# Two-layer hybrid decoder on one core: order of work at the borders of its stages, rewritten

## The chip, the cores and the metric

The kernel runs on one core of a Trainium2 chip. The metric is the device time of one execution in microseconds (us). The engines are TensorE (PE; its weight loads are PEld), VectorE (DVE), ScalarE (ACT), GpSimd (POOL) and SyncE (SP), which issues most of the transfers.

## The reference

Two layers act on 512 tokens of width 1024; inputs and output are float32.

```
for l in range(2):
    x = x + 0.5 * swiglu(rmsnorm(x, ffn1_norm[l]), ffn1_w13[l], ffn1_w2[l])
    z = rmsnorm(x, mix_norm[l]) @ w_in[l]     # pool input | mLSTM q,k,v,o,i,f | attention q,k,v | 3 gates
    y_a = pooling(z); y_b = mLSTM(z); y_c = differential attention(z), with rope tables from positions
    x = x + (sum_b sigmoid(gate_b) * (y_b @ P_b)) @ w_out[l]
    x = x + 0.5 * swiglu(rmsnorm(x, ffn2_norm[l]), ffn2_w13[l], ffn2_w2[l])
return rmsnorm(x, final_norm)
swiglu(h, w13, w2) = (silu(g) * u) @ w2, with g, u = split(h @ w13); the hidden width is 2816 = 22 tiles of 128
```

## The kernel before

x lies in eight tiles of 128 channels by 512 tokens. Every large product is made of three matmuls in a float32 form of reduced precision (`k3`, L341 to L343: hi by hi, hi by lo, lo by hi). So each tile of weights that a transfer brings is split in two: the high part is a cast on ACT (L264), the low part a subtraction on DVE (L265). `weight` hands out the next weight in TensorE's order, splits those that are due within 7 us of TensorE's time, and starts the loads of those due within 16 us (L252 and L257 issue them on SP's queue). Split weights lie in the tiles w (plain), V (forms, below) and dh, dl (down projection, loaded to dr).

There are four FFNs. TensorE's order in one is written out by `ffn_plan`. Of the 22 hidden tiles the first five are plain pairs ("u": a product with g's weights, one with u's). From the sixth on, a pair is computed on halves of the token range and of the weights with seven products instead of eight ("a" to "d", `pair_a` to `pair_d`). Their weights are sums and differences of g's and u's weights (`f1` to `f4`, made by the additions L287 on DVE and then split). Between the pairs lie the products with w2 of the part of hidden tiles before ("D", which update x at L741). The last FFN ends with "E", `finish`: two halves of the tokens, each normed and sent out while the other is computed.

An RMSNorm goes like this. Each updated tile of x is split (L439 on ACT, L440 on DVE) and squared (L452 on ACT), and the squares are added up on POOL (L453, seven additions per norm). TensorE sums over channels (L469), POOL takes the power -1/2 (L461), TensorE spreads the result over the partitions (L516), and ACT copies it to R (L502). The products are started with the unnormed x, and R is multiplied in afterwards: `plain_pair` does so for g (L661), applies silu (L662), does so for u (L665), multiplies u by g on POOL (L666), and splits the result (L651 on ACT, L652 on DVE). R also makes the operands of the forms (`operands`, L479 to L483).

`pair_a` copies its products out of PSUM on ACT (L677, L680). The third block of a pair reuses the PSUM tile that L677 empties.

`tables` makes the rope tables, a mask and the attention's lambdas once, at the end of the first FFN: some 30 operations, most of them on DVE (L573 to L639), issued in one go. The mixer weaves its own small steps between products with w_in; `merge_stream` takes the sigmoids of the gates (L1212) and splits y (L1218 on ACT, L1219 on DVE) before the products with P_b.

TensorE's order is as written. The order on the other engines is chosen when the program is built, from priorities (splits of weights have a high one) and estimated times. At the start, `WARM` matmuls on constants (L544) run ahead of the first weight.

Of the kernel before, what the change touches and what calls it, by code (L numbers as in the profile page):

```python
# [41 lines left out]
WARM = 12  # L42
# [5 lines left out]
PARTS = ((0, 5), (5, 10), (10, 14), (14, 18), (18, 22))  # L48
# [4 lines left out]
def ffn_plan(end):  # L53
# [17 lines left out]
    plan.append(("x", 0, 0))  # L71
# [43 lines left out]
class Trunk:  # L115
# [3 lines left out]
    def __init__(self, ctx, tc, a, out):  # L119
# [7 lines left out]
        self.plan = None  # L127
# [115 lines left out]
    def load_weight(self, i):  # L243
# [4 lines left out]
        if kind in ("p", "d"):  # L248
            _, nk, n = src.shape
            raw = self.wtile() if kind == "p" else self.t([P, 640], "dr", 3)  # L250
            raw = raw[:, : nk * n].rearrange("p (k n) -> p k n", k=nk)
            self.nc.sync.dma_start(raw, src)  # L252
            self.wraw[i] = raw
        elif kind == "f1":
            for c in ("u", "g"):
                raw = self.wtile()
                self.nc.sync.dma_start(raw.rearrange("p (k n) -> p k n", k=KD), src[c])  # L257
                src[c] = raw

# [55 lines left out]
    def weight(self):  # L315
# [10 lines left out]
        for k, at in ahead:  # L326
            if at < 7.0:
                self.split_weight(k)
        for k, at in ahead:
            self.load_weight(k)  # L330
# [53 lines left out]

    def behind(self, ins):
# [46 lines left out]
    def split_x(self, m, gcol, dve=False):  # L432
        nc = self.nc
        g = self.vec[:, gcol + m : gcol + m + 1]
        xh, xl = self.act(dt=F32R), self.act(dt=F32R)
        if dve:
            nc.vector.tensor_scalar(out=xh, in0=self.x[m], scalar1=g, scalar2=None, op0=ALU.mult)
        else:
            nc.scalar.activation(xh, self.x[m], AF.Copy, scale=g)  # L439
        nc.vector.scalar_tensor_tensor(  # L440
            out=xl, in0=self.x[m], scalar=g, in1=xh.bitcast(F32), op0=ALU.mult, op1=ALU.subtract
        )
        self.xs[m] = (xh, xl)

    def square(self, m):
# [7 lines left out]
        nc.gpsimd.tensor_tensor(out=self.ssq, in0=self.ssq, in1=sq, op=ALU.add)  # L453
# [68 lines left out]
    def setup(self):  # L522
# [25 lines left out]
        for m in range(KD):  # L548
            self.split_x(m, V_FFN1, m % 2 == 0)
            if m == 0:  # L550
# [3 lines left out]
        self.split_weight(1)  # L554

    def tables(self):

        nc, a, c = self.nc, self.a, self.const

# [3 lines left out]
        def load(out, in_):  # L563
            self.order(nc.gpsimd.dma_start(out, in_), self.last_pool)
# [16 lines left out]
        self.mqb = self.t([P, P], "mqb", dt=BF16)  # L581
        self.behind(nc.vector.tensor_copy(self.mqb, mq[:, :P]))
# [4 lines left out]
        lv = lam.rearrange("p (l i d) -> p l i d", l=L * 2, i=2)  # L587
        self.behind(nc.vector.tensor_tensor(out=pr, in0=lv[:, :, 0, :], in1=lv[:, :, 1, :], op=ALU.mult))
        sm = self.t([P, L * 2], "lsum")
# [13 lines left out]
        ang = y()  # L603
        self.behind(nc.vector.tensor_copy(ang, pos))
        nc.vector.tensor_scalar(out=ang, in0=ang, scalar1=c[:, C_INV : C_INV + 1], scalar2=None, op0=ALU.mult)
# [8 lines left out]
        n1, n2, s1, kk = y(), y(), y(), y()  # L614
        nearest(n1, ang, 2.0**-20)
        axpy(ang, n1, -(2.0**20), ang)
        nearest(n2, ang, 2.0**-9)
        axpy(ang, n2, -(2.0**9), ang)
        nc.vector.tensor_scalar(out=s1, in0=n1, scalar1=BIG_1, scalar2=None, op0=ALU.mult)
        axpy(s1, n2, MID_1, s1)  # L620
        nc.vector.tensor_tensor(out=kk, in0=s1, in1=ang, op=ALU.add)
        nearest(kk, kk, 1.0 / TWO_PI)
        axpy(s1, kk, -PI_1, s1)
        nc.vector.tensor_tensor(out=ang, in0=ang, in1=s1, op=ALU.add)
        axpy(ang, kk, -PI_2, ang)
        axpy(ang, n2, MID_2, ang)
        axpy(ang, n1, BIG_2, ang)
        nc.vector.tensor_scalar(out=s1, in0=n1, scalar1=BIG_3, scalar2=None, op0=ALU.mult)
        axpy(s1, n2, MID_3, s1)
        axpy(s1, kk, -PI_3, s1)  # L630
        nc.vector.tensor_tensor(out=ang, in0=ang, in1=s1, op=ALU.add)
        nc.vector.tensor_scalar(out=ang, in0=ang, scalar1=PI_F, scalar2=-PI_F, op0=ALU.min, op1=ALU.max)
        self.cos = self.t([P, T], "cos")
        self.sin = self.t([P, T], "sin")
        nc.scalar.activation(s1, ang, AF.Sin)
        nc.vector.tensor_scalar(out=self.sin, in0=s1, scalar1=c[:, C_SGN : C_SGN + 1], scalar2=None, op0=ALU.mult)
        nc.scalar.activation(kk, ang, AF.Sin, scale=0.5)
        nc.scalar.activation(kk, kk, AF.Square)
        nc.vector.tensor_scalar(out=self.cos, in0=kk, scalar1=-2.0, scalar2=1.0, op0=ALU.mult, op1=ALU.add)  # L639
# [15 lines left out]
    def plain_pair(self, xs, act):  # L655
# [59 lines left out]
    def ffn(self, gnext, extra=None):  # L715
# [6 lines left out]
        for kind, p, j in ffn_plan(gnext == V_FIN):  # L722
            if kind == "u":
                yield from self.plain_pair(xs, acts[0])
            elif kind == "a":
                pairs[j] = yield from self.pair_a()
# [6 lines left out]
            elif kind == "x":  # L733
                if extra is not None:
                    extra()
# [390 lines left out]
    def pool_mix(self, l, c):  # L1126
        nc = self.nc
        pw = self.t([P, P], "pw", 2)
        nc.sync.dma_start(pw, self.a["pool_w"][l, c])
# [77 lines left out]
    def merge_stream(self, l):  # L1207
        nc = self.nc
        for m in range(KD):
# [5 lines left out]
        ys = []  # L1215
        for c in range(KD):
            yh, yl = self.act(dt=F32R), self.act(dt=F32R)
            nc.scalar.copy(yh, self.y[c])  # L1218
# [176 lines left out]
```

## Time and profile before

| | us |
|---|---|
| median of 3 runs | 2291.49 |
| lowest, highest | 2288.96, 2293.58 |
| the profiled execution | 2286.44 |
| its span, first to last instruction | 2284.6 |
| TensorE busy | 2218.4 (97%) |
| VectorE busy | 1581.7 (69%) |
| ScalarE busy | 1020.4 (45%) |
| GpSimd busy | 234.0 (10%) |
| mean granted clock of TensorE | 0.988 |

The table is of one profiled execution but for its first two lines; that execution lies 0.2% below the median. TensorE's granted clock is 1 at 2.4 GHz and 0.5 at 1.2 GHz.

### The profile page before, as it was taken

The page shows a single profiled execution, that of the slowest core. Times are in us where ns is not written, and L with a number is a line of the kernel's source. Part 1 is how long each engine was busy: PE and PEld are TensorE (multiplying, and loading weights), DVE is VectorE, ACT ScalarE, POOL GpSimd, SP SyncE. Part 2 cuts the span into 40 slices and gives each one's busy share as a digit, 9 for nine tenths or more (in the row PEclk, how much of TensorE's full clock was granted, in tenths as well). Part 3 has the DMA queues.
Part 4 walks back from the last instruction along what each step waited for, and adds up shares of the span by engine and source line. Part 5 has one row for each costly group of instructions (what it writes and reads, how often), then busy time and mean ns, then how long its engine had stood idle before and what let it go on. Part 6 is the DMA issues. An engine that isn't in the chain of part 4 may idle for free. (4 is left out here: it accounts for less than half of the span.)

```text
span 2284.6 us, 33195 instructions
## 1 busy us (share of the span) xinstructions
PE 2218.4 (97%) x13116; PEld 1944.4 (85%) x13116; DVE 1581.7 (69%) x2426; ACT 1020.4 (45%) x1717; POOL 234.0 (10%) x183
## 2 busy tenths in 40 slices
PE   8999998999999999999999999999999999999997
PEld 6899997887787888999988999988887778899997
DVE  6876777757845577777677777665686465877775
ACT  4444453534453344444443444454344534444444
POOL 3100002001201320000020000010120032100002
PEclk8999999999999999999999999999999999999999
DMA  4333331313222333333224333222222223333323
GB/s 154 122 100 100 98 102 35 97 60 106 83 81 79 122 105 117 109 95 100 83 85 131 99 103 97 84 62 84 84 92 83 83 96 108 126 105 97 101 70 102
DMA packets 76524, 219.43 MB, mean 96 GB/s; under 512 B 9256, under 2 KB 11832, under 8 KB 76368
## 3 DMA queue, kind: packets, MB, share of 16 engines
q1 hardware_dynamic: 73648, 214.29, 30.0%
q10 hardware_dynamic: 2496, 2.43, 0.3%
q8 instruction: 102, 1.67, 0.3%
q0 software_dynamic: 224, 0.60, 0.1%
q14 instruction: 54, 0.44, 0.1%
HBM read 210.97 MB, written 2.11 MB: 93 GB/s over the span
## 5 line engine op out<-in xcount | busy, mean ns | idle before, releaser
L341 PE MATMUL mx<-A,V 128*128 128x256 f32 x1632 | 457.0, 280 | 11.7 <-ACT A L677 11.7
L343 PE MATMUL mx<-A,V 128*128 128x256 f32 x1632 | 457.8, 280 | 1.4 <-DVE V L265 1.3
L341 PE MATMUL mm<-A,w 128*128 128x512 f32 x1120 | 450.9, 403 | 7.2 <-DVE x L741 3.7
L342 PE MATMUL mx<-A,V 128*128 128x256 f32 x1632 | 456.2, 280 | 0.0
L342 PE MATMUL mm<-A,w 128*128 128x512 f32 x1120 | 440.5, 393 | 4.1 <-DVE A L1219 1.9
L343 PE MATMUL mm<-A,w 128*128 128x512 f32 x1120 | 441.0, 394 | 2.0 <-DVE w L265 2.0
L265 DVE TENSOR_TENSOR V<-w,V 128x1024 fp32r<-128x1024 f32 (+1 forms) x272 | 295.5, 1105 | 159.1 <-PE mx L342 96.8
L264 ACT CAST V<-w 128x1024 fp32r<-128x1024 f32 (+1 forms) x272 | 256.5, 943 | 272.3 <-issue 98.0
L341 PEld LDWEIGHTS mx<-A,V 128*128 128x128 f32 x1632 | 306.3, 188 | 17.6 <-ACT A L677 12.5
L342 PEld LDWEIGHTS mx<-A,V 128*128 128x128 f32 x1632 | 307.9, 189 | 4.4
L343 PEld LDWEIGHTS mx<-A,V 128*128 128x128 f32 x1632 | 307.5, 188 | 2.0 <-DVE V L265 2.0
L264 ACT CAST w<-w 128x1024 fp32r<-128x1024 f32 (+2 forms) x166 | 172.4, 1039 | 295.5 <-PE mm L342 94.2
L265 DVE TENSOR_TENSOR w<-w,w 128x1024 fp32r<-128x1024 f32 (+2 forms) x166 | 209.8, 1264 | 107.4 <-ACT w L264 107.0
L342 PE MATMUL mm<-A,dh 128*128 128x512 f32 (+1 forms) x736 | 281.0, 382 | 2.5 <-DVE A L652 2.5
L343 PE MATMUL mm<-A,dl 128*128 128x512 f32 (+1 forms) x736 | 279.9, 380 | 0.9 <-DVE dl L265 0.8
L341 PE MATMUL mm<-A,dh 128*128 128x512 f32 (+1 forms) x736 | 280.6, 381 | 0.0
L341 PEld LDWEIGHTS mm<-A,w 128*128 128x128 f32 x1120 | 213.1, 190 | 52.3 <-ACT w L264 4.2
L342 PEld LDWEIGHTS mm<-A,w 128*128 128x128 f32 x1120 | 213.1, 190 | 49.7 <-DVE A L1219 3.6
L343 PEld LDWEIGHTS mm<-A,w 128*128 128x128 f32 x1120 | 212.2, 189 | 48.1 <-DVE w L265 2.5
L264 ACT CAST dh<-dr 128x512 fp32r<-128x512 f32 (+1 forms) x168 | 111.0, 661 | 244.4 <-PE mm L342 117.9
L741 DVE SCALAR_TENSOR_TENSOR x<-mm,x 128x512 f32<-128x512 f32 x152 | 104.5, 688 | 121.3 <-PE mm L343 121.3
L343 PEld LDWEIGHTS mm<-A,dl 128*128 128x128 f32 x736 | 138.4, 188 | 28.3 <-DVE dl L265 1.7
(236 smaller groups left out, 3272.8 us busy)
## 6 DMA issues: line engine op xcount, KB each, us to landing
w<-in_w13a SPq DMA_DIRECT2D x88, 512.0 KB, 3.5
w<-in_w13b SPq DMA_DIRECT2D x88, 512.0 KB, 3.4
w<-in_w_fm SPq DMA_DIRECT2D x76, 512.0 KB, 3.4
dr<-in_w2b SPq DMA_DIRECT2D x56, 256.0 KB, 2.6
dr<-in_w2a SPq DMA_DIRECT2D x48, 256.0 KB, 2.6
dr<-in_w2a SPq DMA_DIRECT2D x32, 320.0 KB, 2.9
dr<-in_w2b SPq DMA_DIRECT2D x32, 320.0 KB, 2.9
w<-in_w_p SPq DMA_DIRECT2D x16, 512.0 KB, 3.4
```

The lines of the kernel that those rows point to most:

```text
L264: self.last_hi = nc.scalar.copy(hi, raw)
L265: self.last_lo = nc.vector.tensor_tensor(out=lo, in0=raw, in1=hi.bitcast(F32), op=ALU.subtract)
L341: nc.tensor.matmul(ps, wh, xh, start=start, stop=False, skip_group_check=more)
L342: nc.tensor.matmul(ps, wh, xl, start=False, stop=False, skip_group_check=more)
L343: nc.tensor.matmul(ps, wl, xh, start=False, stop=stop, skip_group_check=more)
L741: nc.vector.scalar_tensor_tensor(out=self.x[m], in0=ps, scalar=0.5, in1=self.x[m], op0=ALU.mult, op1=ALU.add)
```

## The change

It has these parts, and leaves the arithmetic as it was but for where it is done.

1. `WARM` goes from 12 to 20.
2. `PARTS` goes from parts of 5, 5, 4, 4, 4 hidden tiles to 5, 4, 4, 4, 5.
3. `weight` looks up to 23 us ahead: while a plain weight is used, forms due within 13 us are split and those due within 23 us loaded. Of plain and down weights no more than two at a time, the one in use among them, are split, and no more than three loaded.
4. All loads of weights are tied to one order, that of use (`fetch`); the pooling weights' load comes behind the last of them.
5. The sums of squares (`square`) and the product u by g of a plain pair (`take_u`) move from POOL to DVE.
6. At the start, the first weight's low part comes behind three tiles of x instead of five, and the last ones behind it (`order`).
7. `tables` becomes a generator whose steps are issued at least 1.6 us of TensorE's planned time apart, from the first pair of the last part on, instead of at once behind the last pair.
8. `merge_stream` splits y before it takes the sigmoids.

```diff
-WARM = 12
+WARM = 20
-PARTS = ((0, 5), (5, 10), (10, 14), (14, 18), (18, 22))
+PARTS = ((0, 5), (5, 9), (9, 13), (13, 17), (17, 22))
-    plan.append(("x", 0, 0))
+    def fetch(self, out, in_):
+
+        d = self.nc.sync.dma_start(out, in_)
+        if self.last_load is not None:
+            self.order(d, self.last_load)
+        self.last_load = d
...
-        ahead, at = [], self.pe_time(i)
+        kind = self.wsrc[i][0]
+        plain = kind == "p"
+        split, load, at = [], [], self.pe_time(i)
+        seen = {"p": 0, "d": 0}
+        seen[kind] = 1
         for k in range(i + 1, len(self.wsrc)):
-            if at > 16.0:
+            if at > 23.0:
                 break
-            ahead.append((k, at))
+            nxt = self.wsrc[k][0]
+            if nxt in ("p", "d"):
+                seen[nxt] += 1
+                if at < 7.0 and seen[nxt] <= 2:
+                    split.append(k)
+                if at < 16.0 and seen[nxt] <= 3:
+                    load.append(k)
+            else:
+                if at < (13.0 if plain else 7.0):
+                    split.append(k)
+                if at < (23.0 if plain else 16.0):
+                    load.append(k)
             at += self.pe_time(k)
...
+    def steps(self, gen, us=1.6):
+
+        if next(gen, self) is not self:
+            self.defer(us, lambda: self.steps(gen, us))
...
-        nc.gpsimd.tensor_tensor(out=self.ssq, in0=self.ssq, in1=sq, op=ALU.add)
+        nc.vector.tensor_tensor(out=self.ssq, in0=self.ssq, in1=sq, op=ALU.add)
...
-            self.split_x(m, V_FFN1, m % 2 == 0)
-            if m == 0:
+            self.split_x(m, V_FFN1, m % 2 == 0, self.last_lo if m > 2 else None)
+            if m == 2:
                 self.split_weight(0)
...
+        yield
         nearest(n1, ang, 2.0**-20)
+        yield
         axpy(ang, n1, -(2.0**20), ang)
+        yield
...
             nc.vector.tensor_tensor(out=u, in0=ps, in1=self.R, op=ALU.mult)
-            self.last_pool = nc.gpsimd.tensor_tensor(out=u, in0=u, in1=g, op=ALU.mult)
+            nc.vector.tensor_tensor(out=u, in0=u, in1=g, op=ALU.mult)
             self.gated(u, g, act)
...
             elif kind == "a":
+                if extra is not None and j == PARTS[-1][0]:
+                    self.steps(extra())
...
     def merge_stream(self, l):
         nc = self.nc
+        ys = []
+        for c in range(KD):
+            yh, yl = self.act(dt=F32R), self.act(dt=F32R)
+            nc.scalar.copy(yh, self.y[c])
+            nc.vector.tensor_tensor(out=yl, in0=self.y[c], in1=yh.bitcast(F32), op=ALU.subtract)
+            ys.append((yh, yl))
         for m in range(KD):
             for br in range(3):
                 g = self.gates[m, br]
```

The lines behind the changed ones move down: L265 becomes L271, L287 becomes L293, L661, L665 and L666 become L722, L726 and L727, L652 becomes L713, L741 becomes L801, and L608, L609 and L612 become L651, L652 and L655. Three places show what the change moves on DVE.

In the first FFN, where the plain pairs end, DVE's rows before are these: the last pair's R multiplied in (L661, L665), with the forms' sums (L287) and low parts (L265, tiles V) around them, up to the split of the last pair (L652).

```order
L661 TENSOR_TENSOR V_569<-mm_578,R_272 128x512
L287 TENSOR_TENSOR w_608<-w_608,w_574 128x512
L265 TENSOR_TENSOR V_605<-w_574,V_605 128x512
L287 TENSOR_TENSOR w_574<-w_574,w_576 128x512
L265 TENSOR_TENSOR V_612<-w_608,V_611 128x1024
L287 TENSOR_TENSOR w_576<-w_574,w_608 128x512
L265 TENSOR_TENSOR V_654<-w_574,V_653 128x1024
L287 TENSOR_TENSOR w_759<-w_663 128x512
L665 TENSOR_TENSOR V_569<-mm_617,R_272 128x512
L287 TENSOR_TENSOR w_759<-w_759,w_661 128x512
L265 TENSOR_TENSOR V_708<-w_576,V_707 128x1024
L652 TENSOR_TENSOR A_645<-V_569,A_644 128x512
```

At the same place after the change, from the last pair's g on:

```order
L722 TENSOR_TENSOR V_581<-mm_596,R_280 128x512
L726 TENSOR_TENSOR V_581<-mm_636,R_280 128x512
L271 TENSOR_TENSOR V_625<-w_490,V_624 128x1024
L713 TENSOR_TENSOR A_578<-V_483,A_577 128x512
L293 TENSOR_TENSOR w_962<-w_840 128x512
L271 TENSOR_TENSOR V_734<-w_492,V_733 128x1024
L293 TENSOR_TENSOR w_962<-w_962,w_838 128x512
L727 TENSOR_TENSOR V_581<-V_581 128x512
L713 TENSOR_TENSOR A_664<-V_581,A_663 128x512
```

The sums and low parts of the first forms now stand ahead of the last pair's g; between u (L726) and the product u by g (L727), which POOL did before, stand five other rows.

In the second FFN the same place was before as in the first, but for one addition (L287) that stood ahead of L661. After the change DVE's rows there, again from the last pair's g on, are these:

```order
L722 TENSOR_TENSOR V_7710<-mm_7725,R_7377 128x512
L271 TENSOR_TENSOR V_7754<-w_7642,V_7753 128x1024
L293 TENSOR_TENSOR w_7919<-w_7763 128x512
L726 TENSOR_TENSOR V_7710<-mm_7765,R_7377 128x512
L293 TENSOR_TENSOR w_7919<-w_7919,w_7761 128x512
L727 TENSOR_TENSOR V_7710<-V_7710 128x512
L271 TENSOR_TENSOR V_7863<-w_7644,V_7862 128x1024
L713 TENSOR_TENSOR A_7793<-V_7710,A_7792 128x512
```

Here only one row (L293) stands between L726 and L727.

In the last part of the first FFN, DVE's rows after the change have the tables' steps (L651, L652, L655; tiles cos and sin serve as scratch) among the pairs' work; before, all of them stood behind the last pair, among the last updates of x and their splits.

```order
L713 TENSOR_TENSOR A_2897<-A_2677,A_2896 128x512
L651 TENSOR_SCALAR A_2839<-cos_2775 128x512
L271 TENSOR_TENSOR V_2942<-w_2938,V_2941 128x1024
L652 TENSOR_SCALAR A_2839<-A_2839 128x512
L801 SCALAR_TENSOR_TENSOR x_8_78<-mm_2905,x_8_78 128x512
L655 SCALAR_TENSOR_TENSOR cos_2775<-A_2839,cos_2775 128x512
L271 TENSOR_TENSOR V_3001<-w_2821,V_3000 128x1024
L667 TENSOR_SCALAR sin_2776<-A_2838 128x512
L762 TENSOR_TENSOR A_2844<-A_2844,mm_2947 128x256
L293 TENSOR_TENSOR w_3269<-w_3157 128x512
```

One or two steps of the tables now stand between every two pieces of the pairs' work.

## Rows read from the trace of the kernel before

**Rows 1.** The page's first part: busy time, share of the span and instructions of each engine.
```profile
PE 2218.4 (97%) x13116; PEld 1944.4 (85%) x13116; DVE 1581.7 (69%) x2426; ACT 1020.4 (45%) x1717; POOL 234.0 (10%) x183
```

**Rows 2.** The waits of PE: line, for what; us in total, times, longest.
```profile
PE mx L341 <- ACT A L677: 11.7, 4, 4.1
PE mm L341 <- ACT A L821: 5.8, 2, 2.9
PE mm L341 <- DVE x L741: 3.7, 1, 3.7
...
PE mx L341 <- ACT A L1218: 3.0, 2, 1.6
PE mm L341 <- DVE mif L801: 3.0, 4, 1.3
...
PE mx L469 <- POOL A L1263: 2.9, 1, 2.9
```

**Rows 3.** Windows of half clock: us; PE, PEld, DVE, ACT, POOL busy; PEclk, DMA, GB/s.
```profile
10.50:17.30 6.80, 4.77 (x12) 3.65 (x12) 6.73 (x9) 5.07 (x9) 1.55 (x1) 0.50 0.76 293
27.60:34.40 6.80, 6.08 (x18) 5.17 (x19) 1.33 (x2) 1.04 (x1) 2.64 (x2) 0.50 0.33 109
85.60:89.00 3.40, 3.40 (x16) 3.40 (x17) 2.72 (x6) 1.51 (x3) 0.00 (x0) 0.50 0.65 155
...
389.40:396.20 6.80, 6.80 (x21) 5.54 (x21) 1.31 (x2) 0.08 (x1) 1.96 (x1) 0.50 0.21 62
...
sum 44.20, PE 41.45 PEld 35.89 DVE 25.54 ACT 22.57 POOL 7.42; mean PE 4.15 PEld 3.59 DVE 2.55 ACT 2.26 POOL 0.74
```

**Rows 4.** Timeline of the start: start, us, instruction [idle before <- releaser].
```profile
9.92 0.50 PE L341 MATMUL mm<-A,w 128*128 128x512 f32 x1 [3.30 <-ACT w L264]
...
12.70 0.80 PE L343 MATMUL mm<-A,w 128*128 128x512 f32 x1 [2.03 <-DVE w L265]
...
15.75 12.51 POOL L453 TENSOR_TENSOR ssq<-ssq,A 128x512 f32<-128x512 f32 x7 [14.49 <-ACT A L452]
...
19.89 2.31 DVE L265 TENSOR_TENSOR w<-w,w 128x1024 fp32r<-128x1024 f32 x1
...
36.67 0.59 ACT L502 COPY R<-mx 128x512 f32<-128x512 f32 x1 [6.62 <-PE mx L516]
```

**Rows 5.** Timeline of the first FFN's border from plain pairs to forms.
```profile
77.36 0.68 DVE L265 TENSOR_TENSOR V<-w,V 128x512 fp32r<-128x512 f32 x1
78.08 0.69 DVE L287 TENSOR_TENSOR w<-w,w 128x512 f32<-128x512 f32 x1
78.69 1.22 DVE L265 TENSOR_TENSOR V<-w,V 128x1024 fp32r<-128x1024 f32 x1
79.82 0.68 DVE L287 TENSOR_TENSOR w<-w,w 128x512 f32<-128x512 f32 x1
...
82.99 1.58 POOL L666 TENSOR_TENSOR V<-V 128x512 f32<-128x512 f32 x1 [8.72 <-DVE V L665]
...
84.60 0.62 ACT L651 CAST A<-V 128x512 fp32r<-128x512 f32 x1 [2.96 <-POOL V L666]
...
85.54 0.56 PE L341 MATMUL mx<-A,V 128*128 128x256 f32 x1 [4.14 <-ACT A L677]
```

**Rows 6.** Timeline of the same border in the third FFN.
```profile
1205.15 0.69 DVE L287 TENSOR_TENSOR w<-w 128x512 f32<-128x512 f32 x1 [1.62 <-DMA w<-in_w13a]
...
1215.26 0.48 PE L341 MATMUL mx<-A,V 128*128 128x256 f32 x1 [4.13 <-ACT A L677]
```

**Rows 7.** Windows from R to the border and around the tables, columns as in rows 3.
```profile
37.30:76.60 39.30, 39.30 (x175) 32.53 (x174) 35.49 (x59) 20.04 (x31) 8.33 (x4) 1.00 0.31 108
297.00:356.00 59.00, 58.69 (x397) 54.04 (x396) 41.06 (x66) 26.42 (x44) 1.61 (x3) 1.00 0.30 92
356.00:390.00 34.00, 27.55 (x110) 20.86 (x109) 31.25 (x50) 17.32 (x28) 11.85 (x12) 0.94 0.08 23
```

**Rows 8.** Timeline of ACT in the first mixer, where TensorE waits for L821.
```profile
450.63 1.04 ACT L264 CAST w<-w 128x1024 fp32r<-128x1024 f32 x1 [6.02 <-PE mm L342]
451.69 1.28 ACT L1047 ACT_TABLE_LOAD   x1
```

**Rows 9.** Timeline of the end: ACT's queue issues stores.
```profile
2267.54 2.80 ACTq L1293 DMA_DIRECT2D out<-A  x4
```

More of the change, by code (lines that the diff above doesn't have):

```diff
@@ L319, in weight @@
         self.split_weight(i)
-        ahead, at = [], self.pe_time(i)
+        kind = self.wsrc[i][0]
[3 more added lines that the diff above has]
+        seen[kind] = 1
         for k in range(i + 1, len(self.wsrc)):
-            if at > 16.0:
+            if at > 23.0:
                 break
-            ahead.append((k, at))
+            nxt = self.wsrc[k][0]
[10 more added lines that the diff above has]
+                    load.append(k)
             at += self.pe_time(k)
[L326 to L329, printed above, removed]
+        for k in split:
+            self.split_weight(k)
+        for k in load:
             self.load_weight(k)
@@ L430, in prep, with split_x @@
         self.square(m)
-    def split_x(self, m, gcol, dve=False):
+    def split_x(self, m, gcol, dve=False, after=None):
         nc = self.nc
@@ L435, in split_x @@
         xh, xl = self.act(dt=F32R), self.act(dt=F32R)
+        vec = []
         if dve:
-            nc.vector.tensor_scalar(out=xh, in0=self.x[m], scalar1=g, scalar2=None, op0=ALU.mult)
+            vec.append(nc.vector.tensor_scalar(out=xh, in0=self.x[m], scalar1=g, scalar2=None, op0=ALU.mult))
         else:
-            nc.scalar.activation(xh, self.x[m], AF.Copy, scale=g)
-        nc.vector.scalar_tensor_tensor(
+            self.last_xh = nc.scalar.activation(xh, self.x[m], AF.Copy, scale=g)
+        vec.append(nc.vector.scalar_tensor_tensor(
             out=xl, in0=self.x[m], scalar=g, in1=xh.bitcast(F32), op0=ALU.mult, op1=ALU.subtract
-        )
+        ))
+        if after is not None:
+            for v in vec:
+                self.order(v, after)
+        self.last_xl = vec[-1]
         self.xs[m] = (xh, xl)
@@ L554, in setup @@
         self.split_weight(1)
+        self.order(self.last_hi, self.last_xh)
+        self.order(self.last_lo, self.last_xl)
     def tables(self):
         nc, a, c = self.nc, self.a, self.const
+        tick = self.t([P, 16], "rsv", 2)[:, 0:1]
+        done = nc.gpsimd.tensor_tensor(out=tick, in0=self.x[0][:, 0:1], in1=self.x[0][:, 0:1], op=ALU.add)
         def y(shape=(P, T), dt=F32):
@@ L563, in load @@
         def load(out, in_):
-            self.order(nc.gpsimd.dma_start(out, in_), self.last_pool)
+            self.order(nc.gpsimd.dma_start(out, in_), done)
         gb = self.t([P, L * 8], "gb")
@@ L602, in tables @@
         load(pos, a["positions"].partition_broadcast(P))
-        ang = y()
+        self.cos = self.t([P, T], "cos")
+        self.sin = self.t([P, T], "sin")
+        ang, s1 = self.cos, self.sin
+        yield
+        yield
         self.behind(nc.vector.tensor_copy(ang, pos))
+        yield
         nc.vector.tensor_scalar(out=ang, in0=ang, scalar1=c[:, C_INV : C_INV + 1], scalar2=None, op0=ALU.mult)
@@ L1128, in pool_mix @@
         pw = self.t([P, P], "pw", 2)
-        nc.sync.dma_start(pw, self.a["pool_w"][l, c])
+        self.order(nc.sync.dma_start(pw, self.a["pool_w"][l, c]), self.last_load)
         pm = self.ps("mx")
@@ L1214, in merge_stream @@
                     self.order(si, e)
[L1215 to L1218, printed above, removed]
-            nc.vector.tensor_tensor(out=yl, in0=self.y[c], in1=yh.bitcast(F32), op=ALU.subtract)
-            ys.append((yh, yl))
         mg = []
```

34 lines of the change are left out of this document (25 added, 9 removed).

## The prediction

> **What bounds the kernel now.** The page's first part comes first: TensorE is busy for 2218.4 us of the span of 2284.6, VectorE for 1581.7, and the others for less than half [rows 1]. So TensorE sets the time, and at most two things can be had without fewer columns: its 66.2 us of idle time (2284.6 less 2218.4), and what the half clock costs it. For the first I read the waits of PE. They are not many small ones: five lines carry the larger part, each with a few long waits [rows 2]. For the second I read windows of the stretches at a granted clock of 0.50, the 1.2 GHz level. Ahead of the tail there are ten, 44.2 us in all [rows 3]; half of that, 22.1 us, is what they cost. Each begins during or behind a wait, or several close together. Then I looked at the places one by one, in the timeline. All lie at borders: the start, the step from plain pairs to forms, the end of the first FFN, the mixer's gates, the merge, and the tail.
>
> **The start and the first border.** Here the chain runs through DVE, so I add up the chain and not the gaps. TensorE waits 3.30 us for the first weight's cast and 2.03 us for its low part [rows 4]; both stretches at half clock, from 10.5 and 27.6, belong here [rows 3]. POOL adds the squares in 12.51 us, 1.79 each, and a DVE operation beside it took 2.31 us where its like takes 1.22 [rows 4, 5]. R is ready at 37.26. What an addition takes on DVE itself the rows of the forms' sums and low parts show, which also read two tiles in SBUF: 0.61 from start to start for 512 columns, 1.13 for 1024 [rows 5]; so an estimate for 256 wide is 0.35 and for 640 wide 0.74. In the change POOL's 12.51 us become seven times 0.61, or 4.3 us, R no longer waits for POOL's sums, and the low part comes two positions earlier. I take R at 28, since the third weight's loads and TensorE's sums still stand ahead of it (27 to 31). The eight further warm matmuls fill the 3.30 us and start nothing earlier; they cost up to 0.2 us.
>
> From R to the last pair's g, the order of the changed kernel has on DVE 43 operations of 512, 7 of 1024, 20 of 256 and 2 of 640: 26.2 + 7.9 + 7.0 + 1.5 = 42.6 us. Before, DVE was busy for 35.49 of 39.30 us there, from 37.3 to 76.6, and POOL for 8.33 [rows 7]; TensorE needs no more than those 39.3, so the stretch is now DVE's. It ends at 70.6. From there to the end of L727 there are five of 512 and two of 1024, 5.3 us, then the cast of the result, 0.5, and the copy L738, 0.3 (starts 84.60, and TensorE going on at 85.54, bound the two at 0.94 [rows 5]). The third block of the first pair would start at 76.8 where it started at 85.54 [rows 5]. That is 8.7; for the bounds, R at 27 and no slip give 10, R at 31 gives 5.7, and a slip on top 5. I take **8**.
>
> **The other borders.** L677 is waited for four times, 11.7 us in all, 4.14 and 4.13 of it in the first and third FFN [rows 2, 5, 6], which leaves 3.4 for the second and fourth. POOL's product there starts 8.72 us after its last (so it is not POOL that is full): it comes late since u's turn on DVE lies behind sums and low parts, and the cast L651 and the copy L677 stand behind it on ACT [rows 5]. In the change, from u on DVE does u, one sum and the product, 3 x 0.61, and ACT's cast and copy 0.9: 2.7 us, against two blocks of twelve matmuls that TensorE has left; sixteen such took 3.40 us at half clock [rows 3], so 24 at full clock take 2.6. The wait goes nearly to nothing: **2.5** of 3.4 (bounds -2 and 3.4; below nothing if the longer look-ahead makes DVE late). In the third FFN the sums began late, as DVE waited 1.62 us for a transfer of g or u [rows 6]; loads up to 23 us ahead take that away. The wait of 4.13 and half of the stretch of 3.4 at half clock behind it are 5.8; I take **5** (2 to 5.8).
>
> **The tables.** From 356 to 390 TensorE is busy for 27.55 of 34 us, so 6.45 are idle, 3.7 of them for x at L741, which stands behind the tables on DVE [rows 2, 7]; two stretches of half clock, 3.4 and 6.8 us [rows 3], cost 5.1. In the last part, 297 to 356, DVE is busy for 41.06 of 59 us [rows 7]. The tables' 27 steps at about 0.61 are 16.5 us: 57.6 of 59. They fit there, barely, among splits that `weight` asks for up to 7 us ahead. What stays is the last x's way through split and square, 1.5 us. I take **10** of 11.5 (6 to 11.5).
>
> **Mixer, merge, tail.** L821 is waited for 2.9 us in each layer [rows 2]: ACT does a cast of 1.04 us and then loads a table, 1.28 us, ahead of it, having been idle for 6.02 us [rows 8]. In the changed order the table's load comes ahead of the cast, in that idle time: 1.3 per layer. The gates' wait for mif, 3.0 in all [rows 2], shrinks by about a microsecond per layer, as DVE takes mif ahead of a low part. Against that, the output of v on DVE (mv) now stands behind two or three reciprocals; I price that at 0.6 per layer. Together **3.5** (-2, if mv is waited for longer, to 8, if all waits and the half clock behind them go). Splitting y first changes less than it says: the cast of y needs free tiles and comes behind the same transfer, and only one moves ahead of one sigmoid; of 3.0 us [rows 2] I take **1** (0 to 2). At the end, four stores hold ACT for 2.80 us [rows 9] and PE waits 2.9 for what is behind them [rows 2]; with five hidden tiles in the last part instead of four a tile of output takes 15 matmuls instead of 12, at 0.11 us each 1.6 instead of 1.3 us, the stores spread out, and **1.8** is won (0 to 2.9). For waits that a new order of loads and splits makes elsewhere I take off **2** (0 to 8).
>
> **The sum.** 8 + 2.5 + 5 + 10 + 3.5 + 1 + 1.8 - 2 = 29.8. Against the profiled execution, 2286.4, that is 2256.6; it stood 5.1 below the median of the runs, so 2261.7, or 2262.
>
> **Rivals.** First, DVE becomes the bound at more than the first border. For it speak 57.6 of 59 us in the last part and 42.6 us behind R; against it, that 42 sums and 20 products on POOL no longer slow DVE beside them, which cost about 1.1 each [rows 4, 5]. If R comes at 31 and DVE is 5 us behind, the first border gives nothing; if the tables exceed 17.9 us (59 less 41.06), low parts of forms come late and 6 of 10 go; with 2 at the other borders 16 are lost: 2278.
>
> Second, the clock falls again behind the waits that are left. In the trace it fell behind 3.30 us of idle time [rows 3, 4] and behind 4.14 [rows 3, 5]; how short a wait leaves it alone no row shown tells, and some of one to two microseconds stay. If the stretches of the first FFN's end and the third border stay, 5.1 and 1.7 are not won: 2269. The Trainium skill, "TensorE: Matmul & The Clock Gate", section "What's actually happening", says that how many matmuls run at the half clock differs from run to run of one kernel, since the monitor's window runs freely; no run here shows it yet, and by it eight further warm matmuls are no promise of a full clock.
>
> Third, it ends slower: all loads of weights now stand in one order on SP's queue, and a load of w2 that waits for a free dr tile, which DVE's low part frees, holds the loads of w13 behind it. With 17 form pairs in each of four FFNs, 68, slower by over 0.2% needs 34.4 us more than my forecast, or 0.51 us for each pair. Against it: in the steady part DMA is at 0.30 and TensorE idle for 0.3 of 59 us [rows 7], so there is slack. I put it at 2300.
>
> Fourth, the change does not do what it says: waits at one border move to the next, since TensorE's order stays; the time stays near 2290.
>
> **How the numbers follow.** Within 0.2%, 4.6 us, counts as the same. The forecast, 2250 to 2268, gets 0.58; the first rival 0.16, the second 0.12, the third 0.07, the fourth 0.07. Faster: 0.58 + 0.16 + 0.12 = 0.86; same 0.07; slower 0.07. The range goes from 2246, where all upper bounds hold (43.6 us), to 2281, which takes in the first two rivals.
>
> **What would show it.** Right: no wait for L453's successor at the first sums of squares; a third block that starts near 77; no x waited for near 375; waits for L738 under a microsecond in the last three FFNs; fewer than six stretches at half clock; the table load of L1107 ahead of a cast. Wrong: waits for low parts of V (L271) in the last part of the first FFN or within the pairs, DVE busy without a pause ahead of them; SP's queue holding w13's loads; waits for mv; half clock behind waits of one or two microseconds.

## The result, and the profile after

The changed kernel takes 2258.92 us in the median of 4 runs (2256.43 to 2260.04), against 2291.92 of before beside it: a ratio of 0.9856, with a 95% interval of 0.9839 to 0.9873. The profiled execution takes 2259.48 us, with a span of 2257.7 us, 26.9 less than before; the medians differ by 33.0, as the profiled execution of the kernel before lay 5.5 us below its median. The forecast was 2262, with 2246 to 2281 as its range.

The page's first part, for [rows 1]: POOL has lost 98 us, DVE gained only 12.4 though it took over 62 operations, and TensorE's busy time fell by 12.8. Most of it is that TensorE runs less at half clock: half of the difference between its busy time in those stretches, 41.45 us before [rows 3] and 18.34 after (below), is 11.6, an estimate.

```profile
PE 2205.6 (98%) x13148; PEld 1937.6 (86%) x13148; DVE 1594.1 (71%) x2488; ACT 1018.0 (45%) x1716; POOL 136.0 (6%) x122
```

The waits of PE in the changed kernel, for [rows 2]; L738 is what was L677, L881 was L821, L1272 was L1218, L483 was L453, L1323 was L1263:

```profile
PE mx L361 <- ACT A L738: 10.5, 4, 7.0
PE mm L361 <- ACT A L881: 7.0, 2, 3.5
...
PE mx L361 <- ACT A L1272: 2.4, 2, 1.6
...
PE mx L499 <- POOL A L1323: 1.0, 1, 1.0
PE mx L499 <- DVE ssq L483: 0.9, 1, 0.9
```

The waits for x and for mif are gone, and so is most of that for POOL at the end. The two largest are still there. L738 has grown at the first border, 7.0 in place of 4.1, and L881 in both layers, 3.5 in place of 2.9.

Windows of the changed kernel's stretches at half clock ahead of the tail, columns as in [rows 3]: five, 23.8 us in all, where there were ten with 44.2.

```profile
74.20:84.40 10.20, 5.70 (x25) 5.62 (x26) 7.69 (x11) 3.10 (x6) 0.00 (x0) 0.50 0.00 0
...
sum 23.80, PE 18.34 PEld 16.96 DVE 16.28 ACT 13.72 POOL 0.00; mean PE 3.67 PEld 3.39 DVE 3.26 ACT 2.74 POOL 0.00
```

To see where the time went I cut both traces at the same matmuls of the written order: the third block of the first pair (first matmul of L341 behind the wait for L677), and the first matmul of each sum of squares (L469) or, for the first mixer, of R's spread (L516). Microseconds of each stage, with those of four experiments told below:

| stage | before | after | old_ahead | ug_pool | tables_once | best_parts |
|---|---|---|---|---|---|---|
| start to third block | 85.54 | 78.70 | 78.53 | 80.58 | 78.64 | 75.00 |
| rest of the first FFN, to R | 311.12 | 301.64 | 300.01 | 300.07 | 304.34 | 298.38 |
| first mixer and merge | 412.79 | 410.78 | 411.91 | 410.05 | 410.93 | 405.85 |
| second FFN | 347.50 | 348.59 | 352.72 | 348.56 | 347.45 | 346.19 |
| third FFN | 351.45 | 347.27 | 351.37 | 354.66 | 347.53 | 346.07 |
| second mixer and merge | 416.29 | 415.01 | 415.53 | 415.02 | 415.25 | 410.46 |
| last FFN, to the final sums | 348.64 | 346.06 | 351.49 | 349.24 | 346.49 | 345.30 |
| end | 11.26 | 9.65 | 10.42 | 9.64 | 10.14 | 10.50 |

### The profile page after: what moved, and what is told of

Its sections match the earlier page's. It is cut to its first block, busy times and chain, and to the rows that moved or that the text cites. A ratio compares the mean times of both kernels' runs of the same rounds, so it can differ in the third digit from the quotient of the medians.

```text
span 2257.7 us, 33170 instructions
## 1 busy us (share of the span) xinstructions
PE 2205.6 (98%) x13148; PEld 1937.6 (86%) x13148; DVE 1594.1 (71%) x2488; ACT 1018.0 (45%) x1716; POOL 136.0 (6%) x122
## 4 chain that ended last, share of the span: by engine, by line
PE 76%; DVE 13%; DMA 5%; ACT 3%; issue 2%; POOL 1%; SPq 0%; ACTq 0%; DVEq 0%; POOLq 0%
PE mm L362 16%; PE mm L361 16%; PE mm L363 16%; PE mx L363 8%; PE mx L362 8%; PE mx L361 8%; DVE w L271 3%; DVE V L271 2%; DMA w<-in_w_p 2%; ACT w L270 2%; DMA w<-in_w_fm 1%; DVE w L293 1%; PE mx L191 1%; PE mx L1141 1%; PE mx L188 1%
## 5 line engine op out<-in xcount | busy, mean ns | idle before, releaser
L271 DVE TENSOR_TENSOR V<-w,V 128x1024 fp32r<-128x1024 f32 (+1 forms) x272 | 291.2, 1089 | 140.0 <-PE mx L362 77.7
L271 DVE TENSOR_TENSOR w<-w,w 128x1024 fp32r<-128x1024 f32 (+2 forms) x166 | 207.2, 1248 | 105.3 <-ACT w L270 104.3
L361 PEld LDWEIGHTS mm<-A,w 128*128 128x128 f32 x1120 | 210.7, 188 | 46.6 <-ACT w L270 2.6
L362 PEld LDWEIGHTS mm<-A,w 128*128 128x128 f32 x1120 | 211.0, 188 | 46.0 <-DVE A L1273 4.0
L363 PEld LDWEIGHTS mm<-A,w 128*128 128x128 f32 x1120 | 210.3, 188 | 46.1 <-DVE w L271 1.1
L801 DVE SCALAR_TENSOR_TENSOR x<-mm,x 128x512 f32<-128x512 f32 x152 | 104.4, 689 | 112.8 <-PE mm L363 112.6
L362 PEld LDWEIGHTS mm<-A,dh 128*128 128x128 f32 x744 | 140.1, 188 | 30.4 <-DVE A L713 9.2
```

The source lines that it names most:

```text
L271: self.last_lo = nc.vector.tensor_tensor(out=lo, in0=raw, in1=hi.bitcast(F32), op=ALU.subtract)
L361: nc.tensor.matmul(ps, wh, xh, start=start, stop=False, skip_group_check=more)
L362: nc.tensor.matmul(ps, wh, xl, start=False, stop=False, skip_group_check=more)
L363: nc.tensor.matmul(ps, wl, xh, start=False, stop=stop, skip_group_check=more)
L801: nc.vector.scalar_tensor_tensor(out=self.x[m], in0=ps, scalar=0.5, in1=self.x[m], op0=ALU.mult, op1=ALU.add)
```

## Three places in the trace after

The timeline of the first border in the changed kernel, DVE, ACT and PE, for [rows 5]:

```profile
68.45 0.39 PE L363 MATMUL mm<-A,w 128*128 128x512 f32 x1
...
72.36 0.69 DVE L726 TENSOR_TENSOR V<-mm,R 128x512 f32<-128x512 f32 x1
72.96 1.22 DVE L271 TENSOR_TENSOR V<-w,V 128x1024 fp32r<-128x1024 f32 x1
74.09 0.69 DVE L713 TENSOR_TENSOR A<-V,A 128x512 fp32r<-128x512 f32 x1
74.69 0.69 DVE L293 TENSOR_TENSOR w<-w 128x512 f32<-128x512 f32 x1
75.30 1.23 DVE L271 TENSOR_TENSOR V<-w,V 128x1024 fp32r<-128x1024 f32 x1
76.43 0.69 DVE L293 TENSOR_TENSOR w<-w,w 128x512 f32<-128x512 f32 x1
77.03 0.69 DVE L727 TENSOR_TENSOR V<-V 128x512 f32<-128x512 f32 x1
...
77.76 0.62 ACT L712 CAST A<-V 128x512 fp32r<-128x512 f32 x1 [3.78 <-DVE V L727]
78.28 0.36 ACT L738 COPY A<-mx 128x256 f32<-128x256 f32 x1
...
78.70 0.58 PE L361 MATMUL mx<-A,V 128*128 128x256 f32 x1 [7.04 <-ACT A L738]
```

The first row is TensorE's last matmul of the last u; DVE takes that u only at 72.36, 3.5 us after it has ended. Then TensorE, ACT and the copy L738 wait for one product on DVE (L727), and ahead of it DVE works without a pause, mostly on forms that are due later. L738 does not read this product: the block that it copies had ended at 70.3, and it stands behind the cast L712 in ACT's order. No run puts it ahead of that cast. The window from R to this u shows how full DVE is in the whole stretch: the third busy time, DVE's, is 42.55 of 43.02 us. (The first busy time, 42.32, is TensorE's; it takes in the first two blocks of the forms, which come behind the last u.)

```profile
29.34:72.36 43.02, 42.32 (x199) 35.33 (x197) 42.55 (x72) 24.28 (x36) 0.00 (x0) 1.00 0.46 163
```

ACT's timeline in the first mixer of the changed kernel, and PE's first matmul behind it, for [rows 8]:

```profile
428.02 1.28 ACT L1107 ACT_TABLE_LOAD   x1
431.33 0.21 ACT L1107 ACTIVATE g_thr<-g_thr 128x16 f32<-128x16 f32 x1 [2.03 <-DVE g_thr L1106]
433.42 1.04 ACT L270 CAST w<-w 128x1024 fp32r<-128x1024 f32 x1 [1.87 <-DMA w<-in_w_fm]
434.37 1.56 ACT L881 ACTIVATE A<-mm,rT 128x256 f32<-128x256 f32 x4
...
434.89 0.39 PE L361 MATMUL mm<-w,A 128*128 128x256 f32 x1 [3.45 <-ACT A L881]
```

The table's load lies in idle time, as forecast. But the cast ahead of L881 now waits for its transfer, and the four copies that TensorE waits for stand behind it.

DVE's timeline at the second FFN's border, and PE:

```profile
843.62 0.69 DVE L293 TENSOR_TENSOR w<-w 128x512 f32<-128x512 f32 x1 [1.98 <-DMA w<-in_w13b]
844.23 0.68 DVE L726 TENSOR_TENSOR V<-mm,R 128x512 f32<-128x512 f32 x1
...
847.15 0.38 PE L361 MATMUL mx<-A,V 128*128 128x256 f32 x1 [2.20 <-ACT A L738]
```

It is the same pattern: a sum for a later form stands ahead of u on DVE and waits 1.98 us for a load.

## Experiments: undoing one part

All are the changed kernel with the edit shown (its main lines); ratios are to the kernel before, on the same chip, and that of the changed kernel is 0.9856 (0.9839 to 0.9873). The intervals of tables_ssq, old_parts, old_ahead and ug_pool lie above that one, and those of dv_first and best_parts, further down, below it. The other runs' intervals meet it, so what they show is read from the stages of their traces and not from the ratio.

**tables_once**: `ffn` calls the tables behind the last pair again.

```diff
+    plan.append(("x", 0, 0))
...
-                if extra is not None and j == PARTS[-1][0]:
-                    self.steps(extra())
...
+            elif kind == "x":
+                if extra is not None:
+                    for _ in extra():
+                        pass
```

> The changed kernel with the tables issued at once behind the last pair, as before. Theory: the spread of the tables is worth about 10 us, the largest single term, so 2266 to 2271 us, and x is waited for again near 355 for 3 to 4 us with half clock behind. Rival: the five hidden tiles of the last part or the squares on DVE had taken the wait away already, and it is 2258 to 2263 us.

0.9875 (0.9861 to 0.9890), 2261.23 us. A wait for x comes back, but the rest of the first FFN loses only 2.7 us (table). So the spread alone is not the ten.

```profile
PE mm L362 <- DVE x L804: 2.8, 1, 2.8
```

**ssq_pool**: the squares' additions on POOL.

```diff
-        nc.vector.tensor_tensor(out=self.ssq, in0=self.ssq, in1=sq, op=ALU.add)
+        nc.gpsimd.tensor_tensor(out=self.ssq, in0=self.ssq, in1=sq, op=ALU.add)
```

> The changed kernel with the additions of the squares back on POOL. With the tables at once the changed kernel lost only 2.6 us by the end of the first FFN, not 10. Theory now: most of that term came from the squares, since POOL's additions of 1.3 to 1.8 us slowed DVE beside them and came last before L499; so by the end of the first FFN 4 to 6 us go, and some 5 us more at the start, where R again waits for seven additions on POOL: 2265 to 2271 us. Rival: the parts of 5 hidden tiles at the end did it, and only the start loses: 2261 to 2264.

0.9888 (0.9873 to 0.9902), 2263.74 us. The start loses 3.0 us (third block at 81.66), and then nothing: the rest of the first FFN takes 301.75 us, where the changed kernel takes 301.64. The theory of that expectation fell. The run gives something else: R's spread came 3.1 us later, at 30.71 for 27.63, and the third block 3.0 later. In both, 51 us lie between the two, as in tables_once (27.55, 78.64).

**tables_ssq**: both edits at once.

> The changed kernel with both the tables at once behind the last pair and the squares' additions on POOL. Alone, the first cost 2.6 us by the end of the first FFN and the second nothing there (its 3 us went at the start). Theory: each of the two takes the same wait away, since the last x is late only when the tables' operations on DVE are slowed by POOL beside them; with both undone the wait of 3 to 4 us for x and those for the last split come back with half clock behind, 9 to 13 us by the end of the first FFN: 2270 to 2276 us. Rival: the two add up, 6 us: 2264 to 2267.

0.9895 (0.9879 to 0.9912), 2265.95 us. The rest of the first FFN takes 306.00 us, 4.4 more than after the change, where the two edits alone gave 2.7 and 0.1. The time lies in the range of the rival, which added the two up; the stage shows that they do not add up. The waits of PE from 360 to 392 are for the same three things as in the kernel before, in other shares (there 3.7 for x, 1.7 for its split, 0.6 for dl):

```profile
PE mm L363 <- DVE A L467: 3.3, 3, 1.9
PE mm L362 <- DVE x L804: 1.5, 1, 1.5
PE mm L364 <- DVE dl L272: 1.4, 1, 1.4
```

L467 is the split of x on DVE. To compare the stage without the clock I take off half of what lies in it at half clock: 6.83 us before, 2.87 after, 3.24 in tables_once, 2.78 in ssq_pool and 1.67 here. That leaves 304.3 before, 298.8 after, 301.1 and 299.0 with one edit undone, and 304.3 with both: all of the waits of before. So the two do overlap, as the theory has it: 2.3 and 0.2 us alone, 5.5 together. The 9 to 13 us of the theory were wrong since the clock did not fall behind these waits, 6.2 us in all, where it did before; why not I can't tell.

**old_parts**: parts of 5, 5, 4, 4, 4.

```diff
-PARTS = ((0, 5), (5, 9), (9, 13), (13, 17), (17, 22))
+PARTS = ((0, 5), (5, 10), (10, 14), (14, 18), (18, 22))
```

> The changed kernel with parts of 5, 5, 4, 4, 4 hidden tiles. Theory: the tail loses the 1.8 us that PE waited for behind the stores, and the last part of the first FFN, which is shorter by a fifth, gets the tables denser, so 1 to 3 us go there: 2259 to 2264 us. Rival: the parts do the work that the tables' term was given, and 5 us or more go by the end of the first FFN: over 2264.

0.9888 (0.9874 to 0.9903), 2263.14 us. The tail is as forecast: PE waits 2.85 us for L1323 again, for 1.03, and the end loses 2.0 us (11.66). The last FFN loses 5.3 more (351.34), which was not forecast: its border waits 2.75 us for 0.42, with 3.4 us at half clock behind. The first FFN was mistaken: it does not lose but gains 4.6 us (third block at 77.09, rest 298.70). R's spread came 0.7 us later there and the third block 1.6 earlier.

**old_ahead**: the old look-ahead in `weight`.

```diff
         for k in range(i + 1, len(self.wsrc)):
-            if at > 23.0:
+            if at > 16.0:
                 break
...
+        for k, at in ahead:
+            if at < 7.0:
+                self.split_weight(k)
+        for k, at in ahead:
             self.load_weight(k)
```

> The changed kernel with the look-ahead of weight as before: 7 us for splits and 16 for loads, no limit of a kind. Theory: the third border waits about 4 us again and half clock follows, and the first border waits longer by the two sums that then come after it (2 to 4 us), while the cast that waits for a transfer ahead of L881 moves back: 2260 to 2268 us. Rival: the order of loads and DVE's lighter load were enough, and it is 2255 to 2260.

0.9924 (0.9908 to 0.9941), 2271.94 us: the largest loss of all, and more than forecast. The second, third and last FFN lose 4.1, 4.1 and 5.4 us (table), each at its border. In the second, DVE makes the first forms only when the last u is due (TensorE stops at 844.28), and u, L712, comes behind them:

```profile
844.17 1.22 DVE L271 TENSOR_TENSOR V<-w,V 128x1024 fp32r<-128x1024 f32 x1
845.31 0.68 DVE L712 TENSOR_TENSOR V<-mm,R 128x512 f32<-128x512 f32 x1
...
847.75 0.58 PE L347 MATMUL mx<-A,V 128*128 128x256 f32 x1 [3.47 <-ACT A L724]
```

The first border, where 2 to 4 us were to go, did not lose (78.53). In the mixers L881 (L867 here) is waited for 2.9 us per layer, as before the change and as forecast, but two waits that the change had taken away are back:

```profile
PE mm L347 <- DVE mif L847: 3.0, 4, 1.3
PE mx L1036 <- DVE g_lf L1031: 2.3, 2, 1.1
```

**ug_pool**: the product of u and g on POOL.

```diff
-            nc.vector.tensor_tensor(out=u, in0=u, in1=g, op=ALU.mult)
+            nc.gpsimd.tensor_tensor(out=u, in0=u, in1=g, op=ALU.mult)
```

> The changed kernel with the product u by g of the plain pairs back on POOL. Theory: at the first border DVE is full, so taking 5 x 0.6 us off it and giving it back POOL's slowing (about 1.1 us for each product) comes out even there; at the other borders the product takes 1.6 us on POOL instead of 0.6 on the path: 1 us more at each, 2258 to 2263 us. Rival: DVE as the bound gains more than POOL costs, and the first border's wait shrinks from 7 to 3 or 4 us: 2253 to 2256.

0.9917 (0.9903 to 0.9932), 2269.95 us: some 11 us lost where at most 4 were expected. The third FFN is 7.4 us slower than after the change and 3.2 slower than before. POOL takes 2.68 us for the product while DVE splits beside it, and half clock comes with the wait:

```profile
1195.10 2.68 POOL L727 TENSOR_TENSOR V<-V 128x512 f32<-128x512 f32 x1 [11.66 <-DVE V L726]
...
1197.82 0.62 ACT L712 CAST A<-V 128x512 fp32r<-128x512 f32 x1 [3.62 <-POOL V L727]
...
1198.76 0.58 PE L361 MATMUL mx<-A,V 128*128 128x256 f32 x1 [4.21 <-ACT A L738]
```

So in the third FFN, with the other parts as changed, the look-ahead without the product on DVE costs 3.2 us, the product without the look-ahead gives 0.1, and both together give 4.2.

**warm12_ylast**: 12 warm matmuls, and the sigmoids ahead of y's split.

```diff
-WARM = 20
+WARM = 12
...
+        for m in range(KD):
+            for br in range(3):
+                g = self.gates[m, br]
+                si = nc.scalar.activation(g, g, AF.Sigmoid)
+                for e in self.exps[-2:]:
+                    self.order(si, e)
         ys = []
         for c in range(KD):
...
-                si = nc.scalar.activation(g, g, AF.Sigmoid)
```

> The changed kernel with 12 warm matmuls and with the sigmoids ahead of y's split; the two places lie 680 us apart, so the trace tells them apart. Theory: neither matters on its own; the first sums of squares start within 1 us of where they did, though a stretch at half clock may come at about 12 us, and the waits of the merge stay at 3.5 to 4.5 us per layer: 2256 to 2261 us. Rival: without the eight matmuls the clock falls at the start, R comes 2 to 3 us later, and the first border, which hangs on R through DVE, moves by as much: 2260 to 2264.

0.9866 (0.9850 to 0.9882), 2259.28 us. The start at half clock comes back (6.8 us from 9.4), but R's spread is only 1.0 us later, and the third block too (79.67). The mixers with their merges take 410.29 and 415.24 us, as after the change. Neither part shows in the time.

**free_loads**: the forced order of loads taken out of `fetch`.

```diff
-        if self.last_load is not None:
-            self.order(d, self.last_load)
```

> The changed kernel without the forced order of the loads of weights. Theory (my third rival turned round): the order costs nothing that can be measured, since SP's queue has slack, and 2256 to 2261 us comes out; the loads of w2 may again stand ahead of those of w13 at the start, which would cost R up to 5 us. Rival: loads that wait for free tiles hold others behind them, and without the order the waits for a transfer ahead of L738 and L881 go: 2250 to 2254.

0.9861 (0.9845 to 0.9876), 2258.38 us: no difference. That rival is settled, for this kernel.

## Experiments: mending the two places

**prod_first**: where the plain pairs end, the sums and low parts of forms are tied behind the last product on DVE.

```diff
+            if self.fence is not None:
+                self.order(self.last_lo, self.fence)
...
+            if last:
+                for made in self.made:
+                    self.order(made, prod)
+                self.fence = prod
```

> The changed kernel, but at each border from plain pairs to forms the sums and low parts of the forms that stand between L726 and L727 on DVE come behind L727 (the third form's sum apart). Theory: the wait of 7.04 us at the first border is made by what stands ahead of L727 on DVE, 1.2 us of sums ahead of u and 4.1 us between u and the product; so the third block starts near 74.8 instead of 78.70, a gap of about 3, the half clock behind it is shorter or the same, and the waits of 2.20, 0.81 and 0.42 us at the other three borders go under 0.5: 2251 to 2255 us. Rival: DVE is full over the whole stretch behind R, so the forms' low parts that are put off are waited for instead (L271, tiles V) and the time stays at 2257 to 2261.

0.9840 (0.9823 to 0.9856), 2252.56 us. Its profiled run shows the wait at 3.05 us, no half clock behind it, and the third block at 74.93:

```profile
73.05 1.04 ACT L271 CAST V<-w 128x1024 fp32r<-128x1024 f32 x1 [1.51 <-DVE w L298]
74.00 0.61 ACT L722 CAST A<-V 128x512 fp32r<-128x512 f32 x1
74.52 0.36 ACT L752 COPY A<-mx 128x256 f32<-128x256 f32 x1
...
74.93 0.39 PE L371 MATMUL mx<-A,V 128*128 128x256 f32 x1 [3.05 <-ACT A L752]
```

The start and the rest of the first FFN take 74.93 and 298.35 us, 7.1 less than after the change. No low part is waited for in return. But the other three borders wait 0.76, 1.10 and 0.76 us (2.20, 0.81 and 0.42 after the change), not under 0.5 as expected. And by the ratio the gain is not clear of noise, since the interval meets that of the changed kernel; it rests on the rows.

**dv_first**: the cast of the next weight comes behind the copies L881.

```diff
+        if self.dv_last is not None:
+            if self.dv_skip:
+                self.dv_skip = False
+            else:
+                self.order(self.last_hi, self.dv_last)
...
-                    nc.scalar.activation(out, ps, AF.Copy, scale=self.rT[:, b : b + 1])
+                    self.dv_skip, self.dv_last = True, nc.scalar.activation(out, ps, AF.Copy, scale=self.rT[:, b : b + 1])
```

> The changed kernel, but on ACT the cast of the next weight comes behind the four copies L881 of each pair of value products; one row moves in each layer. Theory: TensorE waits 3.45 and 3.55 us there since that cast stands ahead of the copies and itself waits 1.87 us for a transfer; without it the copies follow the gate's exponential at 431.5, the waits fall to 0.6 to 1 us, and the stretches of 3.4 us at half clock behind them go: 2249 to 2253 us. Rival: the copies are held by the exponential's input, or the cast that now comes later is waited for by TensorE in its place, and the time stays at 2257 to 2261.

0.9821 (0.9806 to 0.9835), 2248.30 us. The copies follow the exponential, the cast is late and hurts nobody:

```profile
431.34 0.22 ACT L1114 ACTIVATE g_thr<-g_thr 128x16 f32<-128x16 f32 x1 [2.16 <-DVE g_thr L1113]
431.47 1.55 ACT L888 ACTIVATE A<-mm,rT 128x256 f32<-128x256 f32 x4
433.33 1.05 ACT L271 CAST w<-w 128x1024 fp32r<-128x1024 f32 x1 [0.31 <-DMA w<-in_w_fm]
...
431.98 0.38 PE L368 MATMUL mm<-w,A 128*128 128x256 f32 x1 [0.53 <-ACT A L888]
```

The two mixers take 406.07 and 410.13 us, 4.7 and 4.9 less: 3 us of the wait, and the half clock behind it, which is gone in both layers.

**both_first**: both edits.

> Both edits, product first and copies first. If the places are independent, as they lie 350 us apart, the gains add up: 2242 to 2248 us. If a later transfer gives one of them back, it is no better than the better of the two.

0.9832 (0.9818 to 0.9847), 2251.19 us: no better than dv_first. The mixers keep their gain (405.75, 409.81), but the first border waits for 4.79 us. On ACT the row of the fourth form's cast stands ahead of the product's, as in prod_first, but the sum that it waits for came later on DVE:

```profile
74.41 1.04 ACT L272 CAST V<-w 128x1024 fp32r<-128x1024 f32 x1 [3.25 <-DVE w L305]
75.36 0.61 ACT L729 CAST A<-V 128x512 fp32r<-128x512 f32 x1
75.88 0.36 ACT L759 COPY A<-mx 128x256 f32<-128x256 f32 x1
```

The first border is not all of it: the other three wait for 1.89 us each, more than in prod_first.

**best_parts**: both edits, that cast tied behind the pair's first copy, and old_parts' parts in all FFNs but the last.

```diff
+                self.order(self.last_hi, self.gate_first or self.gate_cast)
...
+    parts = PARTS_END if end else PARTS
```

> The changed kernel with the product and the copies first, as in the run of both, with the first copy of the first pair ahead of the cast of the fourth form on ACT, and with the parts of before in all FFNs but the last. Theory: in the run of both the first border waited for 4.79 us instead of 3.05 since that cast came ahead of the product's own; with this mended the first border waits for 2 to 3 us, the others for less than 1, the copies for 0.5, and the parts of before give some 3 us in the first FFN: 2238 to 2245 us, faster than all others. Rival: as the waits go, loads come late and half clock returns elsewhere, and it stays at 2247 to 2251.

0.9762 (0.9744 to 0.9779), 2235.51 us, the fastest, and below the 2238 that were forecast at best: 0.0094 below the changed kernel's ratio, or some 21 us. PE's largest waits are now these:

```profile
PE mx L385 <- DVE A L1308: 4.0, 4, 1.2
PE mm L385 <- DVE A L736: 2.8, 9, 0.3
PE mx L384 <- ACT A L1307: 2.5, 2, 1.6
...
PE mx L384 <- ACT A L767: 1.9, 1, 1.9
```

L1307 and L1308 split y, L767 is the border's copy, L736 splits a plain pair's result. Only one border, the first, is waited at; the largest waits left lie in the merge. The run changes the cast's place and the parts at once, so the shares of the two are not shown.

## Why the prediction was right, and which terms were not

**Start and first border: 8 forecast, 6.8 measured.** The chain through DVE was right step by step. From R's first use, at 29.34, to the last u, at 72.36, it took 43.0 us for 42.6 worked out; from there to the end of L727 5.4 for 5.3; then 1.0 for 0.8. Only R came 1.3 us later than the 28 taken. That DVE and not TensorE sets this time is shown by the u that waited 3.5 us for DVE's turn, and by prod_first, where moving rows on DVE brings the third block 3.8 us forward. ssq_pool and warm12_ylast do not tell the two apart: the third block moved with R by 3.0 and 1.0 there, but TensorE's last matmul ahead of the wait moved by as much. Of the 8.0 us by which R's spread comes earlier (35.58 before, 27.63 after) the squares on DVE give 3.1 (ssq_pool); part 6 of the change was undone in no run, and what it gives stays open. What I left out is the price behind it: the wait of 7.04 us came with 10.2 us at half clock, 4.5 of them within the wait, where 3.4 had been [rows 3].

**The tables: 10 forecast, 9.5 measured** in the rest of the first FFN. The size was right, its owner not: I gave all of it to the spread. 5.5 us are waits that the spread and the squares on DVE take away, with an overlap of 3 us (tables_ssq). The other 4.0 us are half clock: 5.1 less at the end of the stage, 1.2 more behind the first border. The spread also has a price that I had put at nothing. Soon after its steps begin, TensorE waits for a sum on DVE (L769) with a step of the tables (L655) and a form's sum ahead of it:

```profile
296.95 0.69 DVE L655 SCALAR_TENSOR_TENSOR sin<-A,sin 128x512 f32<-128x512 f32 x1
297.56 0.68 DVE L293 TENSOR_TENSOR w<-w,w 128x512 f32<-128x512 f32 x1
298.16 0.41 DVE L769 TENSOR_TENSOR A<-A,mx 128x256 f32<-128x256 f32 x1
...
298.63 0.39 PE L361 MATMUL mx<-A,V 128*128 128x256 f32 x1 [1.69 <-DVE A L769]
```

This wait, of 1.0 to 1.7 us, is there in every run with the spread and the new parts, and in none with the tables at once (tables_once, tables_ssq) or with the parts of before in this FFN (old_parts, best_parts). So it is the larger part of the 2.9 us that the new parts cost in this stage (298.70 in old_parts); 0.9 of them are half clock.

**The second and last border: 2.5 forecast.** The last FFN gave 2.6 us up to the final sums, with the end's new shape in it; the second lost 1.1. Of the waits, the second border's grew from 1.73 us to 2.20 and the last one's shrank from 1.70 to 0.42. The failed step is that from u on DVE there would be only u, one sum and the product: a sum ahead of u waits for a load. It does not in every run: with the same rows on DVE there, the sum waited 1.98 us after the change, 0.66 in ssq_pool and not at all in tables_once and dv_first, and TensorE 2.20, 0.50, 0.15 and 0.14. So the second FFN is not worse by rule; why the load is late in some runs stays open. **The third border: 5 forecast, 4.2 measured**, but old_ahead and ug_pool show that the load's earlier start is not enough; it takes the product on DVE as well.

**The mixers and merges: 3.5 and 1 forecast, 3.3 measured** (2.0 in the first layer, 1.3 in the second). The step for L821 was wrong. The table's load did move into idle time, but this took nothing off, since the next row on ACT waits for a transfer; dv_first shows that row to be the whole of the wait but 0.53 us. What was won came from mif (3.0 us before [rows 2]) and from g_lf (2.3 before, which I had not priced), neither of them waited for any longer; old_ahead, where both are back, shows that the look-ahead did it. The 0.6 us per layer for mv do not show: mv is waited for nowhere. Splitting y first gave nothing, against my 1. **The tail: 1.8 forecast, 1.6 measured**; old_parts shows that the last part's size does it.

**The rivals.** DVE did become the bound, but at the first border, as in the forecast, and elsewhere only for single rows (1.7 us at L769, 2.2 at the second border); prod_first shows that even there the order of rows is 4.0 of the 7.04 us. The clock did fall again, for 23.8 us in place of 44.2, and not at the first FFN's end or the third border, the places of that rival. In both merges it fell behind waits of 0.8 to 1.6 us close together, as before the change; this sign of being wrong, half clock behind waits of one or two microseconds, did come. At the start it fell from 12.1 on in prod_first, from 12.8 in old_parts and not at all in the changed kernel, though the same instructions run there in the same order up to then; R's spread came 0.2 and 0.7 us later in those two (27.86 and 28.34 for 27.63). The Trainium skill ("TensorE: Matmul & The Clock Gate", "What's actually happening") says that the number of matmuls at the half clock at a kernel's start changes from run to run; the three traces agree with that, but they are of three kernels. The order of the loads cost nothing (free_loads).

**The sum.** Cut at the stages, the terms come to 26.9 us for 29.8. Every term was 0.2 to 1.2 us too high, and the 2 taken off for new waits made up for part of it. By the medians the gain is 33.0. So it is in part luck that 2262 lies so near 2258.92: at the second border and in the mixers the amounts came about in another way than I said. The lower end of the range was added up wrongly: the 43.6 us of all upper bounds lead to 2248, not 2246.

## What to carry to other kernels

Look at what stands ahead of the awaited row on its own engine. In each of the three places left, a row for later work was the one that made TensorE wait, twice because it waited for a transfer of its own; moving one row per layer was worth 9.6 us by the two mixers' stages. Ask the same of the work that is spread: a step of the tables now stands ahead of a sum that TensorE waits for. Work out a chain through the engine that is full, and not the sum of TensorE's gaps. And undo parts in pairs: here the look-ahead and the moved product were each worth nothing or a loss in the third FFN without the other, and 4.2 us together.

## What had not been expected

A wait's price on this kernel is more than its length: 3.45 and 3.55 us at L881 cost 4.7 and 4.9, with the half clock behind. And the edit made for the mixer (both_first beside prod_first) changed the order of DVE's rows in the first FFN, 350 us earlier, where it cost 1.7 us of waiting: what the scheduler does elsewhere has to be read again after each edit.
